# Forgetting attention with the softmax weights stationary: a single-product maximum pass, row sums from ones columns, and a turned result

## The chip, the cores and the metric

The kernel runs on one core of one Trainium2 chip. The metric is the device time of one execution in microseconds (us). The kernel before took 2423.89 us, the median of 3 runs (2420.24 to 2425.25). Differences of about 0.2% (5 us) are what a measurement of this kernel can tell from no change.

## The reference

One encoder layer over 2048 positions of width 1024. After a norm and one input projection, half of the columns go to a gated MLP over blocks of positions and half to eight attention heads of 64 dimensions. Then come an output projection, a norm, a feed-forward layer with a causal convolution of width 3, and a last norm. The change touches only the attention:

```python
def forgetting_attention(q, k, v, f_logit):
    ...
    c = jnp.cumsum(jax.nn.log_sigmoid(f_logit.astype(jnp.float32)), axis=1)
    ...
        s = jnp.einsum('bhtd,bshd->bhts', qi, k, preferred_element_type=jnp.float32) * scale
        s = s + ci[..., :, None] - c[:, :, None, :]
        s = jnp.where(kpos[None, :] <= qpos[:, None], s, -jnp.inf)
        p = jax.nn.softmax(s, axis=-1)
        return jnp.einsum('bhts,bshd->bthd', p.astype(v.dtype), v)
```

A query sees the keys up to itself. The logit is the scaled product plus a difference of two cumulative sums.

## The kernel before, in words

**Precision.** Every large product is made from operands split into a high and a low part in the 32-bit TensorE type fp32r (names ending in h or hi, and l or lo). A product then takes two or three matrix products.

**Order of the work.** A main stream of products runs from start to end: the projections (`phase_a`), the output projection (`c_half`, `c_late`), and the two halves of the feed-forward layer (`d_half`, `late_half`, `down`). The main helper `mm3` (line 205) issues its products at line 211, and every one of them gives a credit. When the credits reach a rate (3.5 to 4.4 products), one step of the attention is issued by the generator `b_stream`, with a higher priority. So attention is a second stream that is woven into the first. A scheduler then fixes the order on each engine when the program is built. Where the main stream needs the attention's result for a block of 512 queries, `need(tb)` (line 136) issues all steps still missing, and `load_mix` (line 874) reads that result back from DRAM. There are four blocks of queries, tb = 0 to 3. Blocks 0 and 1 have to be done before the output projection's second block of rows, and block 3 before its last one.

**A piece** is one head h and one block tb. It takes two passes.

- *First pass*, `b_max` (line 752). For each block of 512 keys up to the diagonal and each of the four groups of 128 queries, one step: scores with the queries in rows, by two products. Line 772 has 96 rows of contraction (high parts, the two cumulative sums, and constants), line 773 has 128 rows (the cross terms of high and low parts). DVE takes the minimum along the row (the scores are negated), line 776, or 778 with the mask on the diagonal. ACT takes exponentials against that minimum and adds them up (line 781). At the end the row maximum is put together, and the reciprocal of the row sum (lines 783 to 802). `turn` (line 804) transposes the maxima into rows of the query operand t1.
- *Second pass*, `b_mix` (line 812). For each chunk of 128 keys, one step: scores with the keys in rows and up to 512 queries in columns, by two products (lines 833, 834), the mask on the diagonal (837, DVE), the exponential into e (839, ACT), and its split into ph (844, ACT) and pl (845, DVE). Two or three steps later (`LAG`) the product with the values follows, `pv` (line 819): v, the 128 keys by 64 high and 64 low columns, is stationary. ph and then pl move through it, up to 512 columns each (lines 821, 822), and add to one PSUM bank `o` that holds head dimensions in rows and queries in columns.
- *End of a piece*. The high and low halves of `o` are added (856, 857). For every second head the reciprocals of two heads are broadcast and turned by four transposes (line 864), multiplied in, split and written to DRAM.

A diagonal block has four chunks with 512, 384, 256 and 128 columns. Counted over the program, each of the lines 772, 773, 821, 822, 833 and 834 has 224 products of 512 columns and 32 each of 384, 256 and 128.

**Buffers.** The PSUM bank tags that matter are `s` (3 banks for scores), `o` (1 bank) and `dn` (2 banks). Scores use the `dn` banks as well once `self.more` is set, during the first half of the feed-forward layer.

## Time and profile before

| what | value |
|---|---|
| median of 3 runs | 2423.89 us |
| profiled execution | 2419.3 us, span of its instructions 2417.5 us |
| PE busy (products) | 2392.8 us, 11288 products |
| PEld busy (weight loads) | 1998.3 us |
| DVE busy | 1764.8 us |
| ACT busy | 1355.3 us |
| GpSimd busy | 323.2 us |
| DMA engines | 47.9% of 16 engines' span in the main queue |

Each product on PE comes as two instructions, a weight load (PEld) that puts the stationary operand in place, and the product itself, which streams the moving operand. The trace writes the shape as moving columns, for instance 128x512. Durations of products overlap one another in the trace, so that their sum is longer than the span. What one product costs in a row of products is the distance from its start to the next start, or the distance between the weight loads.

### The profile page before, as it was taken

What the parts mean: (1) busy time and instruction counts of PE and PEld (TensorE: products, weight loads), DVE (VectorE), ACT (ScalarE), POOL (GpSimd) and SP (SyncE); (2) the same over time, 40 slices, a digit from 0 to 9 for tenths busy, and PEclk for the clock granted to TensorE, in tenths of its full rate; (3) what the DMA queues carried; (4) which work ended last, traced back from release to release, by engine and by line L of the source; (5) the groups of instructions that cost most, each with busy time, mean ns of one, the idle gap of its engine ahead of it and who ended that gap; (6) DMA issues with size and microseconds to landing.
All of it is one profiled execution on the core that took longest, in us unless ns stands there. A gap on an engine that the chain in (4) does not pass through costs nothing.

```text
span 2417.5 us, 33292 instructions
## 1 busy us (share of the span) xinstructions
PE 2392.8 (99%) x11288; PEld 1998.3 (83%) x11288; DVE 1764.8 (73%) x3108; ACT 1355.3 (56%) x2652; POOL 323.2 (13%) x315
## 2 busy tenths in 40 slices
PE   9999999999999999999999999999999999999998
PEld 7888888988888888888888888888888888888887
DVE  6447776665568778878878774598888877857875
ACT  4246767644456555767677764365555455454444
POOL 4114140100241221211111101100000000000001
PEclk9999999999999999999999999999999999999999
DMA  8673635668855444555445555312222238438633
GB/s 278 182 241 111 206 100 175 186 192 265 260 191 183 160 163 161 165 173 185 146 151 182 170 195 203 116 53 96 79 86 81 87 96 310 157 99 300 205 118 122
DMA packets 246042, 400.58 MB, mean 166 GB/s; under 512 B 51224, under 2 KB 110744, under 8 KB 244448
## 3 DMA queue, kind: packets, MB, share of 16 engines
q1 hardware_dynamic: 240832, 374.34, 47.9%
q0 software_dynamic: 5040, 24.12, 2.5%
q8 instruction: 89, 1.46, 0.2%
q14 instruction: 81, 0.66, 0.1%
HBM read 304.79 MB, written 93.72 MB: 165 GB/s over the span
## 4 chain that ended last, share of the span: by engine, by line
PE 87%; DMA 2%; DVE 1%; ACT 1%; issue 0%; POOL 0%; POOLq 0%; SPq 0%; ACTq 0%; DVEq 0%
PE mm L211 37%; PE D L1378 16%; PE A L1176 3%; PE A L1178 3%; PE A L1177 3%; PE o L822 3%; PE o L821 3%; PE s L773 2%; PE s L772 2%; PE s L834 2%; PE s L833 2%; PE B L1178 2%; PE B L1177 2%; PE B L1176 2%; PE C L1176 1%; PE C L1177 1%
## 5 line engine op out<-in xcount | busy, mean ns | idle before, releaser
L211 PE MATMUL mm<-tlo,whi 128*128 128x512 f32 x896 | 351.4, 392 | 0.0
L211 PE MATMUL mm<-thi,wlo 128*128 128x512 f32 x896 | 351.1, 392 | 0.0
L211 PE MATMUL mm<-thi,whi 128*128 128x512 f32 x896 | 350.5, 391 | 0.5 <-DVE vn L519 0.5
L211 PE MATMUL mm<-whi,thi 128*128 128x512 f32 (+2 forms) x768 | 275.9, 360 | 6.1 <-DVE vn L519 4.4
L211 PE MATMUL mm<-wlo,thi 128*128 128x512 f32 (+2 forms) x768 | 275.5, 359 | 2.2 <-DVE wlo L164 2.2
L211 PE MATMUL mm<-whi,tlo 128*128 128x512 f32 (+2 forms) x768 | 274.8, 358 | 0.0
L150 POOL TENSOR_SCALAR whi<-raw 128x1024 fp32r<-128x1024 f32 (+3 forms) x114 | 132.4, 1163 | 963.2 <-PE mm L211 741.5
L781 ACT ACTIVATE s<-s,part 128x512 f32<-128x512 f32 (+3 forms) x261 | 154.7, 593 | 145.3 <-DVE part L776 80.6
L211 PEld LDWEIGHTS mm<-thi,whi 128*128 128x128 f32 x896 | 168.4, 188 | 35.2 <-issue 0.7
L211 PEld LDWEIGHTS mm<-thi,wlo 128*128 128x128 f32 x896 | 168.5, 188 | 34.1
L211 PEld LDWEIGHTS mm<-tlo,whi 128*128 128x128 f32 x896 | 168.5, 188 | 33.7
L845 DVE TENSOR_TENSOR pl<-e,ph 128x512 fp32r<-128x512 f32 (+1 forms) x218 | 142.9, 662 | 69.6 <-ACT ph L844 40.5
L211 PEld LDWEIGHTS mm<-whi,thi 128*128 128x128 f32 x768 | 145.9, 190 | 26.3 <-DVE vn L519 4.6
L164 DVE TENSOR_TENSOR wlo<-raw,whi 128x1024 fp32r<-128x1024 f32 (+2 forms) x106 | 135.1, 1276 | 44.0 <-POOL whi L150 43.0
L839 ACT ACTIVATE e<-s 128x512 f32<-128x512 f32 (+1 forms) x222 | 114.5, 530 | 91.8 <-DVE s L837 44.0
L211 PEld LDWEIGHTS mm<-wlo,thi 128*128 128x128 f32 x768 | 145.9, 190 | 22.7 <-DVE wlo L164 3.4
L211 PEld LDWEIGHTS mm<-whi,tlo 128*128 128x128 f32 x768 | 145.9, 190 | 19.3
L844 ACT ACTIVATE ph<-e 128x512 fp32r<-128x512 f32 (+1 forms) x218 | 120.6, 563 | 38.7 <-PE o L821 36.6
L1378 PE MATMUL D<-wh,xh 128*128 128x512 f32 x368 | 140.8, 389 | 1.2 <-DVE xo L1479 1.2
L1378 PE MATMUL D<-wl,xh 128*128 128x512 f32 x368 | 141.4, 389 | 0.0
L1378 PE MATMUL D<-wh,xl 128*128 128x512 f32 x368 | 137.5, 389 | 0.0
L776 DVE TENSOR_REDUCE part<-s 128x1 f32<-128x512 f32 x149 | 98.6, 684 | 20.9 <-PE s L773 19.9
(1858 smaller groups left out, 5850.4 us busy)
## 6 DMA issues: line engine op xcount, KB each, us to landing
raw<-in_w_up_dram SPq DMA_DIRECT2D x72, 512.0 KB
m<-kx SPq DMA_DIRECT2D x134, 256.0 KB
m<-kx SPq DMA_DIRECT2D x160, 136.0 KB
x<-act SPq DMA_DIRECT2D x84, 256.0 KB
v<-vd SPq DMA_DIRECT2D x67, 256.0 KB
raw<-in_w_in_dram SPq DMA_DIRECT2D x28, 512.0 KB
raw<-in_w_out_dram SPq DMA_DIRECT2D x24, 512.0 KB
tw<-in_w_down_dram SPq DMA_DIRECT2D x11, 1024.0 KB
```

Of the source, the lines that this page charges most:

```text
L150: self.cast_ins = self.nc.gpsimd.tensor_scalar(out, in_, 1.0, 0.0, ALU.mult, ALU.add).ins
L164: nc.vector.tensor_tensor(lo, raw, f32(hi), op=ALU.subtract)
L211: self.last_mm = self.nc.tensor.matmul(ps, lhsT=a[k], rhs=b[k], start=i == 0, stop=i == 3 * n - 1).ins
L776: nc.vector.tensor_reduce(dst, ps, axis=AX.X, op=ALU.min)
L781: nc.scalar.activation(ps[:, :n], ps[:, :n], AF.Exp, scale=-1.0, bias=dst, accum_out=ls[:, tt, sb:sb + 1])
L839: nc.scalar.activation(e[:, c], ps[:, c], AF.Exp, scale=-1.0)
L844: nc.scalar.activation(ph[:, c], e[:, c], AF.Copy)
L845: nc.vector.tensor_tensor(pl[:, c], e[:, c], f32(ph[:, c]), op=ALU.subtract)
L1176: mm(ps, lhsT=xh[:, ks], rhs=yh[:, k, :], start=fresh and k == 0, stop=False, **kw)
L1177: mm(ps, lhsT=xh[:, ks], rhs=yl[:, k, :], start=False, stop=False, **kw)
L1178: mm(ps, lhsT=xl[:, ks], rhs=yh[:, k, :], start=False, stop=k == 3, **kw)
L1378: nc.tensor.matmul(bank[t], lhsT=x[i][:, ts], rhs=w[k], start=fresh and j == 0 and i + k == 0, stop=last and i == 1, **kw)
```

## The change

- *First pass*: line 773's product and the load of its operand m2 are gone, and so are line 781's exponentials and everything that made a row sum of them. One product of 96 rows and a minimum are left in each step.
- *Second pass*: the scores are made as before. In `pv` the stationary operand is now a group of 128 queries of ph or pl, and the values move: 130 columns for ph (64 high, 2 of ones, 64 low), 66 for pl (64 high, 2 of ones). Each chunk has up to four groups of queries, so up to eight products where there were two. The ones columns collect the row sum. The result has queries in rows and takes two PSUM banks. The product of pl with the low values, which was in before, is left out.
- *End of a piece*: reciprocals from the ones column, high and low halves added, one multiplication. For every second head the result itself is turned by four transposes.
- *Buffers*: scores 3 banks to 2 (with `dn` 5 to 4), `o` 1 to 2, both for one piece. Two v tiles of fixed place with the ones columns written once (a third when `more` is set). Each load of v is two DMAs.

The core of the diff:

```diff
-    "mm": 2, "tp": 2, "dn": 2, "s": 3, "o": 1,
+    "mm": 2, "tp": 2, "dn": 2, "s": 2, "o": 2,
...
-                nc.tensor.matmul(ps[:, :n], lhsT=t1[0:96, ts], rhs=m1[0:96, :n], start=True, stop=False)
-                nc.tensor.matmul(ps[:, :n], lhsT=t2[:, ts], rhs=m2[:, :n], start=False, stop=True)
+                nc.tensor.matmul(ps[:, :n], lhsT=t1[0:96, ts], rhs=m1[0:96, :n], start=True, stop=True)
...
-                nc.scalar.activation(ps[:, :n], ps[:, :n], AF.Exp, scale=-1.0, bias=dst, accum_out=ls[:, tt, sb:sb + 1])
                 yield
...
+        self.V.append(self.V.pop(0))
+        v = self.V[0]
+        for i in range(2):
+            self.dma(f32(v[:, :, 66 * i:66 * i + 64]),
+                     self.vd[hf][sl, h, 64 * i:64 * i + 64].rearrange("(c p) d -> p c d", p=P))
...
         def pv():
-            sc, c, v, ph, pl = late.pop(0)
-            nc.tensor.matmul(po[:, c], lhsT=v, rhs=ph[:, c], start=sc == 0, stop=False)
-            nc.tensor.matmul(po[:, c], lhsT=v, rhs=pl[:, c], start=False, stop=sc == ns - 1)
+            sc, j, v, ph, pl = late.pop(0)
+            for i in range(j, 4):
+                o, c = po[i // 2][:, i % 2, :], slice(i * P, (i + 1) * P)
+                with self.tc.issue_after(first) if sc == 0 and i % 2 else ExitStack():
+                    ins = nc.tensor.matmul(o, lhsT=ph[:, c], rhs=v[:, 0:130], start=sc == 0 and i % 2 == 0, stop=False,
+                                           skip_group_check=True).ins
+                if i % 2 == 0:
+                    first = ins
+                nc.tensor.matmul(o[:, 0:66], lhsT=pl[:, c], rhs=v[:, 0:66], start=False, stop=sc == 4 * tb + i,
+                                 skip_group_check=True)
...
+        for i, o in enumerate(po):
+            q = slice(2 * i, 2 * i + 2)
+            nc.vector.reciprocal(rr[:, q], o[:, :, 64])
+            nc.scalar.activation(op[:, q, :], o[:, :, 66:130], AF.Copy)
+            nc.vector.tensor_tensor(op[:, q, :], o[:, :, 0:64], op[:, q, :], op=ALU.add)
+        nc.vector.tensor_tensor(op, op, rr.unsqueeze(2).broadcast_to([P, 4, 64]), op=ALU.mult)
```

What stands on an engine in the built program is shown at two places, before and changed. The first place is on PE, in a piece of block tb = 1, where the products with the values of a chunk stand. Names: o is the result bank, ph and pl the split weights, v the values, s a bank of scores, m and t the key and query operands, mm the main stream. Before:

```order
L833 MATMUL s_1248_5477<-t1_49_401,m1_47_399 128x256
L821 MATMUL o_1216_5344<-ph_1221_5355,v_1218_5348 128x512
L822 MATMUL o_1216_5344<-pl_1222_5356,v_1218_5348 128x512
L821 MATMUL o_1216_5344<-ph_1225_5372,v_1218_5348 128x512
L822 MATMUL o_1216_5344<-pl_1226_5373,v_1218_5348 128x512
L834 MATMUL s_1248_5477<-t2_1125_4952,m2_1237_5428 128x256
```

Two chunks stand here with two products each, all 512 wide. The same part of a piece in the changed program, on PE:

```order
L832 MATMUL s_1043_4905<-t2_920_4379,m2_1038_4879 128x384
L815 MATMUL o_1013_4796<-v_52_405,ph_1036_4870 128x130
L815 MATMUL o_1014_4797<-v_52_405,ph_1036_4870 128x130
L819 MATMUL o_1013_4796<-v_52_405,pl_1037_4871 128x66
L815 MATMUL o_1013_4796<-v_52_405,ph_1036_4870 128x130
L819 MATMUL o_1013_4796<-v_52_405,pl_1037_4871 128x66
L819 MATMUL o_1014_4797<-v_52_405,pl_1037_4871 128x66
L815 MATMUL o_1014_4797<-v_52_405,ph_1036_4870 128x130
L819 MATMUL o_1014_4797<-v_52_405,pl_1037_4871 128x66
L831 MATMUL s_1047_4927<-t1_49_401,m1_47_399 128x256
```

One chunk now has eight products of 130 and 66 columns. Each has its own part of ph or pl as the stationary operand; products that read alike differ in the group of queries.

The second place is on PE in the output projection, where the main stream first needs the attention's result for block 1 (operands thi and tlo of the main products mm). Before:

```order
L211 MATMUL mm_1574_7213<-wlo_1452_6774,thi_1441_6749 128x512
L772 MATMUL s_1413_6585<-m1_48_400,t1_50_402 128x128
L773 MATMUL s_1413_6585<-m2_1412_6582,t2_1397_6491 128x128
L211 MATMUL mm_1574_7213<-whi_1451_6773,tlo_1443_6751 128x512
L772 MATMUL s_1414_6594<-m1_48_400,t1_50_402 128x256
L773 MATMUL s_1414_6594<-m2_1412_6582,t2_1397_6491 128x256
L211 MATMUL mm_1567_7159<-whi_1454_6779,thi_1441_6749 128x512
```

The last row is the first product that reads the rows of heads 4 to 7 of block 1. Ahead of it the attention is already in the first pass of block 2, and main products stand between its steps. The same place in the changed program, on PE:

```order
L819 MATMUL o_1156_5453<-v_51_403,pl_1193_5649 128x66
L186 MATMUL s_1210_5730<-ident_58,op_1153_5443 128x128 x4
L778 MATMUL s_1337_6645<-m1_48_400,t1_50_402 128x512
L778 MATMUL s_1338_6653<-m1_48_400,t1_50_402 128x512
L778 MATMUL s_1339_6660<-m1_48_400,t1_50_402 128x512
L778 MATMUL s_1340_6668<-m1_48_400,t1_50_402 128x512
L778 MATMUL s_1341_6676<-m1_47_399,t1_50_402 128x512
L778 MATMUL s_1342_6683<-m1_47_399,t1_50_402 128x512
L778 MATMUL s_1344_6693<-m1_47_399,t1_50_402 128x512
L212 MATMUL mm_1487_7279<-whi_1381_6861,thi_1368_6831 128x512
```

The last heads of block 1 (the transposes of their result, line 186) now stand seven products ahead of the main product that needs them. From there back, over four pieces, no main product stands between the attention's: 24 products of the first pass, 64 of the second pass's scores, 208 with the values, 32 transposes and 3 turns of maxima. A second stretch of the same kind stands ahead of the end of block 3: 12 of the first pass, 64 scores, 232 with the values, 8 transposes and a turn.

More of the change, by code (lines that the diff above doesn't have):

```diff
@@ L28 @@
 BIG = 1e30
+VW = 144
 RATES = [3.5, 4.0, 4.4, 3.6]
@@ L428, in first_keys @@
         def first_keys():
-            banks = [self.til(pp, [P, TB], F32, "mm") for _ in range(2)] + [self.scores([P, TB]) for _ in range(3)]
-            banks.append(self.til(self.bpp, [P, TB], F32, "o"))
+            banks = [self.til(pp, [P, TB], F32, "mm") for _ in range(2)] + [self.scores([P, TB]) for _ in range(2)]
+            banks += [self.til(self.bpp, [P, TB], F32, "o") for _ in range(2)]
             def mms(u, b, k):
@@ L732, in scores @@
     def scores(self, shape):
-        self.nscore = (self.nscore + 1) % 5
-        if self.more and self.nscore > 2:
+        self.nscore = (self.nscore + 1) % 4
+        if self.more and self.nscore > 1:
             return self.til(self.dpp, shape, F32, "dn")
```

57 lines of the change are left out of this document (20 added, 37 removed), and 4 rows, old and new, of the table BUFS.

## The prediction

> **What bounds the kernel now.** The page comes first.
>
> ```profile
> span 2417.5 us, 33292 instructions
> PE 2392.8 (99%) x11288; PEld 1998.3 (83%) x11288; DVE 1764.8 (73%) x3108; ACT 1355.3 (56%) x2652; POOL 323.2 (13%) x315
> PEclk9999999999999999999999999999999999999999
> ```
>
> PE is busy for 99% of the span at the full granted clock. That alone proves little, since products overlap in the trace, so the stretches come next: one with attention woven in, one of 512-column products alone.
>
> ```profile
> core 0: us, PE busy (x) PEld busy (x) DVE busy (x) ACT busy (x) POOL busy (x), PEclk, DMA share, GB/s
> 1000.00:1200.00 200.00, 200.00 (x914) 165.95 (x914) 163.20 (x323) 138.84 (x311) 29.36 (x28) 1.00 0.50 163
> 1600.00:1800.00 200.00, 200.00 (x884) 165.62 (x883) 170.49 (x214) 103.88 (x160) 0.00 (x0) 1.00 0.24 84
> ```
>
> In the second, 200 us for 884 products is 0.226 us each, with no gap. In the first there are 914, because some are narrower. So where attention runs, PE takes product after product, and what the change does to PE's row is what it does to the time. The prices of products of other widths come from the timeline of PE and of the weight loads, at a place where a diagonal block makes them narrow.
>
> ```profile
> 607.19 0.33 PE L833 MATMUL s<-t,m 128*128 128x384 f32 x1
> 607.54 0.28 PE L833 MATMUL s<-t,m 128*128 128x256 f32 x1
> 610.07 0.22 PE L833 MATMUL s<-t,m 128*128 128x128 f32 x1
> 610.13 0.28 PE L834 MATMUL s<-t,m 128*128 128x128 f32 x1
> 607.20 0.19 PEld L834 LDWEIGHTS s<-t,m 128*128 128x128 f32 x1
> 607.37 0.19 PEld L833 LDWEIGHTS s<-t,m 128*128 128x128 f32 x1
> 607.54 0.19 PEld L834 LDWEIGHTS s<-t,m 128*128 128x128 f32 x1
> 607.66 0.19 PEld L211 LDWEIGHTS mm<-whi,tlo 128*128 128x128 f32 x1
> 607.78 0.19 PEld L821 LDWEIGHTS o<-ph,v 128*128 128x128 f32 x1
> 608.01 0.19 PEld L211 LDWEIGHTS mm<-whi,thi 128*128 128x128 f32 x1
> 610.08 0.19 PEld L834 LDWEIGHTS s<-t,m 128*128 128x128 f32 x1
> 610.18 0.19 PEld L211 LDWEIGHTS mm<-whi,tlo 128*128 128x128 f32 x1
> 610.29 0.19 PEld L211 LDWEIGHTS mm<-whi,thi 128*128 128x128 f32 x1
> ```
>
> A load starts when the product before its own starts (607.20 against 607.19). So the distance from one load to the next is the slot of one product: 0.17 us for 384 columns (607.20 to 607.37 and on to 607.54), 0.12 for 256 (607.66, 607.78), 0.23 for 512 (608.01). For 128 columns it is 0.10 and 0.11 (610.08, 610.18, 610.29), and this no longer falls with the columns: half of 0.12 would be 0.06. Below 256 columns the slot is that of the weight load. A longer row of narrow products says the same.
>
> ```profile
> 371.69 1.72 PE L561 MATMUL tp<-vn,sw 128*128 128x128 f32 x14
> 373.16 0.47 PE L833 MATMUL s<-t,m 128*128 128x512 f32 x1
> 373.48 0.39 PE L834 MATMUL s<-t,m 128*128 128x512 f32 x1
> ```
>
> From 371.69 to 373.48 stand 14 products of 128 columns and one of 512: 1.79 - 0.23 = 1.56 us, 0.111 each.
>
> **The sum on PE.** Taken away are line 773's products and those of lines 821 and 822, each 224 of 512 columns and 32 of 384, 256 and 128: 224 x 0.226 + 32 x (0.17 + 0.12 + 0.105) = 50.6 + 12.6 = 63.3 us each. First pass -63.3, values -126.5, together -189.8 us.
>
> Added: a head has 24 full chunks with four groups of queries and four diagonal blocks with 4 + 3 + 2 + 1, so 136 groups, 1088 over eight heads, and 2176 products of 130 or 66 columns. The trace shows none as narrow as 66 and none of this pair. By columns alone (0.226/512 us each) they would take 0.057 and 0.029 us; by the slots above, each takes 0.105 to 0.111. I take 0.110: every product brings its own stationary operand, and the rows at 128 columns show the slot of a load whatever streams. That is 239.4 us (228.5 to 241.5 by the rows). Net on PE: +49.6 us (38.7 to 51.7). The turned result costs nothing here: four transposes for every second head, before and now.
>
> The Trainium skill, in "TensorE: Matmul & The Clock Gate", section "Back-to-back issue gap", gives for a stream of load and product pairs a sustained 81 ns at 128 columns. By it the 2176 would take an estimated 176 us and the sum would be about -14 us. The rows here, at 105 to 111 ns, do not agree, and I go by them.
>
> **Other work that goes or comes.** Line 781's exponentials, the loads of m2 in the first pass (80 of 256 KB) and the row-sum arithmetic were all beside PE: in 1000 to 1200 ACT is busy 139 of 200 us and the DMA engines half. They give nothing. The second DMA for each v (80 more issues on SP's queue, in place of the 80 for m2) and GpSimd's memsets of ones are hidden by the same room; if a v came late, the pv that waits for it would hold every main product queued behind it on PE. Both `o` banks belong to one piece, so the next piece's first pv waits for the small operations of the end, but its first pass and two steps lie between. I take nothing for these.
>
> **Where the cover goes: two stretches of attention alone.** The order shows that with fewer banks for scores the attention falls behind the main stream, and that ahead of the products that need block 1 it stands alone on PE for four pieces. There PE's row is not all that counts, because DVE has more work per piece.
>
> ```profile
> L845 DVE TENSOR_TENSOR pl<-e,ph 128x512 fp32r<-128x512 f32 x143 | 109.3, 770 | 45.5 <-ACT ph L844 33.2 <-PE o L822 10.3 <-ACT e L839 1.5
> L845 DVE TENSOR_TENSOR pl<-e,ph 128x384 fp32r<-128x384 f32 x27 | 15.0, 554 | 5.8 <-PE o L822 2.0 <-PE s L833 1.8 <-ACT ph L844 1.6
> L845 DVE TENSOR_TENSOR pl<-e,ph 128x256 fp32r<-128x256 f32 x28 | 12.7, 452 | 11.9 <-PE o L822 9.2 <-ACT ph L844 2.3
> L845 DVE TENSOR_TENSOR pl<-e,ph 128x128 fp32r<-128x128 f32 x20 | 6.6, 331 | 6.4 <-ACT ph L844 3.4 <-PE o L822 3.0
> L776 DVE TENSOR_REDUCE part<-s 128x1 f32<-128x512 f32 x149 | 98.6, 684 | 20.9 <-PE s L773 19.9
> L778 DVE CUSTOM_DVE_ANT_0 s<-s,mask 128x512 f32<-128x512 f32 x29 | 20.5, 705 | 10.6 <-PE s L773 9.8 <-ACT ln L530 0.4
> L778 DVE CUSTOM_DVE_ANT_0 s<-s,mask 128x128 f32<-128x128 f32 x26 | 7.8, 300 | 3.5 <-PE s L773 3.5
> L778 DVE DVE_READ_ACCUMULATOR2_ANT part<- 128x1 f32 x128 | 17.9, 139 | 0.0
> L837 DVE TENSOR_TENSOR s<-s,maskT 128x128 f32<-128x128 f32 x108 | 30.4, 293 | 22.4 <-PE s L834 21.8
> L807 DVE TENSOR_TENSOR t<-s,rowsel 8x512 fp32r<-8x512 f32 x30 | 20.5, 684 | 2.8 <-PE s L806 1.9
> L195 DVE SCALAR_TENSOR_TENSOR tlo<-dn,cols,thi 128x512 fp32r<-128x512 f32 x16 | 11.7, 744 | 3.4 <-ACT thi L194 3.4
> L789 DVE TENSOR_SCALAR m<-mx 128x4 fp32r<-128x4 f32 x32 | 7.6, 236 | 0.6
> L844 ACT ACTIVATE ph<-e 128x512 fp32r<-128x512 f32 x143 | 89.4, 634 | 12.4 <-PE o L821 10.9 <-DVE st L411 0.4 <-ACT st L191 0.3
> L839 ACT ACTIVATE e<-s 128x512 f32<-128x512 f32 x150 | 87.4, 597 | 59.0 <-PE s L834 31.5 <-DVE s L837 18.0 <-DVE pl L845 4.9
> ```
>
> First stretch, PE: 24 first-pass products 4.9 us, scores 4 x 2 x (5 x 0.226 + 0.395) = 12.2, values 208 x 0.11 = 22.9, 32 transposes and three turns 3.7: 43.7 us. DVE: the 32 pl 20 x 0.770 + 4 x (0.554 + 0.452 + 0.331) = 20.7; 16 masks x 0.293 = 4.7; 16 minima x 0.684 = 10.9; eight masked minima at about 0.64 (mean of 0.705 and 0.300, plus 0.139) = 5.1; six tlo of the main stream's norm x 0.744 = 4.5; three turns x 0.684 = 2.1; four ends of a piece, an estimated 1.5 each from the small rows (0.236 twice, 0.293 twice, and a multiplication near the 0.452 of 256 columns) = 6.0; two splits and two sets of maxima 2.8. Together 56.8 us. ACT has 1.23 us for a full chunk, 25 for the 20 and under 40 if the 12 narrow ones cost as much, so it is not the bound. PE waits 56.8 - 43.7 = 13 us.
>
> Second stretch, ahead of block 3's result: 12 first-pass steps in a row, DVE 8 x 0.684 + 4 x 0.64 = 8.0 us against 2.4 on PE, of which the score banks cover a step or two: 4 us. The two second passes behind it are PE's (1.33 us of PE for a full chunk against 1.23 of ACT and 0.77 of DVE).
>
> First passes that are still woven in: from 1000 to 1200 DVE is busy 163.2 of 200 us. Two steps, one of each pass, are now 2 x 0.81 of main products + 0.45 + 0.90 = 2.97 us, so DVE does 2.42 us in them, less 0.684, 0.77 and about 0.1 of masks leaves 0.43 a step for the main stream. After the change a first-pass step has 0.81 + 0.226 = 1.04 on PE and 0.684 + 0.43 = 1.11 on DVE. The 224 steps of blocks 2 and 3 could cost 224 x 0.07 = 16 us; the second passes give it back and the banks hold about a microsecond, so I take 2.
>
> A wait that goes is the first product with block 1's rows, which waited for its load:
>
> ```profile
> 663.14 0.50 PE L211 MATMUL mm<-whi,thi 128*128 128x512 f32 x1 [1.74 <-DMA thi<-mixh]
> ```
>
> It goes into the first stretch: -2. The sum is 49.6 + 13 + 4 + 2 - 2 = +66.6, on the profiled execution's 2419.3 us: 2486. The median of the runs before is 4.6 us above that execution; I put the forecast at 2487.
>
> **The rivals.**
>
> *Narrow products cost what they stream (faster).* If a load hid behind the loads around it, the 2176 would cost 1088 x (0.057 + 0.029) = 94 us, PE would get -96 us, and with the 17 us of waits the time would be 2340. With a slot between, such as the 81 ns above, it is 2419 - 14 + 15 = 2420. It decides from a slot of 189.8/2176 = 87 ns, or 80 ns with the waits. Against it stands every narrow pair in the rows; for it only that none is a pair of 130 and 66. Chance 0.06, of which 0.05 are beyond the bound.
>
> *No waits.* The stretches overlap better than the sums say, and only PE's row counts: 2419.3 + 38.7 to 51.7, about 2465. For it is that the DVE sum uses means with waits for other engines' memory traffic in them. Chance 0.20.
>
> *DVE becomes the bound in all first passes.* The 16 us are paid in full, and each piece of the first stretch adds a microsecond between passes, because a second pass cannot start before its maximum is turned: 2487 + 14 + 4 + 5 = 2510. For it are the two score banks in place of three; against it, that these steps stand among main products. Chance 0.16.
>
> My forecast has the remaining 0.58.
>
> **How the numbers follow.** The forecast's own range is 2470 to 2500. Reaching to the second and third rival gives 2454 to 2512; the faster case and some of the tails are left out. Faster by over 0.2% (5 us, what a measurement here can tell) 0.05, within it 0.01, slower 0.94.
>
> **What would show it.** Right, if the changed profile has 1216 more products, load distances of 0.105 to 0.11 us within a chunk's eight, and the rows of 130 and 66 columns at the same slot. Right, if PE has gaps of some 13 us in a stretch of about 57 us without main products, released by DVE. Wrong, if those distances are near 0.06, or if the time is off by more than the waits while the slots hold.

## The result, and the profile after

The changed kernel took 2548.87 us (median of 4 runs, 2546.07 to 2551.05), the kernel before 2422.06 us on the same chip (4 runs, 2419.61 to 2425.25). The ratio is 1.0524 (95% interval 1.051 to 1.0539). The forecast was 2487 us with a range of 2454 to 2512: the direction was right, the size was half, and the time lies outside the range. The profiled execution took 2547.18 us, its span 2545.5 us, against 2417.5 before: +128.0 us. One execution of one kernel below (without the late loads, 3087.67 us at a mean granted clock of 0.74, where that kernel's other three have 0.98) is left out of its median and its ratio.

The page of the changed kernel, in the lines that stand first in the prediction:

```profile
span 2545.5 us, 34973 instructions
PE 2495.9 (98%) x12504; PEld 2111.7 (83%) x12504; DVE 1768.5 (69%) x3116; ACT 1135.1 (45%) x1998; POOL 320.7 (13%) x318
PEclk9999999999579999999999999899999999999999
```

There are 12504 products, 1216 more, as counted. The share of PE is as good as before. What is new stands in the third line: in the slices from 636 to 764 us the granted clock is 0.5 and 0.7, and near 1600 us 0.8. Before, it was 0.9 or more in every slice.

The price of a narrow product is read from the weight loads, where full and narrow products take turns at the full clock (start, duration):

```profile
1338.00 0.19 PEld L815 LDWEIGHTS o<-v+_1868_9038,ph+_2337_11239 128*128 128x128 f32 x1
1338.11 0.19 PEld L819 LDWEIGHTS o<-v+_1868_9038,pl+_2338_11240 128*128 128x128 f32 x1
...
1338.78 0.19 PEld L815 LDWEIGHTS o<-v,ph 128*128 128x128 f32 x1
1338.89 0.19 PEld L819 LDWEIGHTS o<-v,pl 128*128 128x128 f32 x1
```

From 1338.00 to 1338.89 stand eight of them, 0.111 us each, whether 130 or 66 columns move. Over the whole trace the median distance between the loads is 0.112 us for both. With 0.1115 the 2176 products take 242.6 us, and PE's row is 242.6 - 189.8 = 52.8 us longer. The rest of the 128.0 us, 75.2, is not in the row.

It is in the two stretches without main products. The view of windows gives, for each, its length, PE busy, DVE busy, ACT busy and the granted clock. The first two rows below are the two stretches, from the first product of attention to the next main product; the other two are those shown of before.

```profile
630.80:722.30 91.50, 81.39 (x332) 67.86 (x330) 50.77 (x122) 39.01 (x80) 0.00 (x0) 0.58 0.38 109
1582.50:1646.10 63.60, 50.11 (x318) 43.50 (x316) 35.48 (x75) 40.58 (x80) 3.48 (x8) 0.83 0.32 94
1000.00:1200.00 200.00, 199.90 (x1050) 170.74 (x1048) 144.95 (x278) 88.25 (x164) 37.38 (x34) 1.00 0.42 138
1600.00:1800.00 200.00, 189.51 (x960) 159.41 (x960) 144.48 (x207) 115.51 (x199) 11.68 (x19) 0.96 0.27 88
```

The first stretch took 91.5 us. By the slots of its products, at full clock, PE needs 44.1 there; DVE is busy for 50.8 and ACT for 39.0. No engine accounts for the length. The second took 63.6 us for 42.5 us of slots. Together the two are 47.4 + 21.1 = 68.5 us longer than their slots. 52.8 + 68.5 = 121.3 of the 128.0 us. Of the 68.5, PE stands idle for 91.50 - 81.39 = 10.1 and 63.60 - 50.11 = 13.5 us; for the other 44.9 it is busy, with products that take longer than their slots. Where attention is woven in (1000 to 1200), PE stays full.

The chain of waits inside the first stretch, its shares by line and its longest loads (start, duration):

```profile
by line: PE o L815 22.3%; PE o L819 15.7%; PE s L831 13.9%; PE s L832 10.4%; DMA m<-kx 8.0%; PE s L778 7.0%; DMA tlo<-mixl 6.1%; DVE part L781 4.5%; DMA t<-cc 2.7%; PE s L186 2.4%; PE dn L186 1.9%; DVE s L783 1.7%; issue 1.6%; DVE op L859 1
...
632.94 4.06 DMA m<-kx
641.71 2.49 DMA t<-cc
675.81 3.27 DMA m<-kx
719.85 5.55 DMA tlo<-mixl
```

Loads of keys (m) and of a query's cumulative sum (t) stand in the chain, 10.7% of 91.5 = 9.8 us. The load of the attention's result (thi and tlo) comes last. The tlo in the last row lands at 725.40, after the stretch; what PE waits for at the end of the two stretches is thi:

```profile
722.31 0.80 PE L212 MATMUL mm<-whi,thi 128*128 128x512 f32 x1 [0.60 <-DMA thi<-mixh]
1646.10 0.80 PE L212 MATMUL mm<-whi,thi 128*128 128x512 f32 x1 [6.62 <-DMA thi<-mixh]
```

The 6.62 us for block 3's result are new. Before, the one wait of PE for such a load was the 1.74 us for block 1's. The remainder of the first stretch's chain is PE's, but at which clock? The load of t at 641.71 shows how the clock goes. On PE:

```profile
642.63 0.42 PE L815 MATMUL o<-v,ph 128*128 128x130 f32 x2
644.33 0.94 PE L778 MATMUL s<-m,t 96*128 96x512 f32 x2 [1.28 <-DMA t<-cc]
```

PE waited 1.28 us for the load, at 644.6 us the granted clock fell to half, and it stayed there for 85.3 us:

```profile
640.00:660.00 20.00, 16.84 (x74) 13.82 (x72) 12.32 (x33) 8.27 (x18) 0.00 (x0) 0.62 0.32 86
660.00:680.00 20.00, 16.38 (x57) 13.13 (x57) 10.80 (x30) 5.01 (x12) 0.00 (x0) 0.50 0.39 116
680.00:700.00 20.00, 20.00 (x79) 18.14 (x79) 7.66 (x17) 11.42 (x23) 0.00 (x0) 0.50 0.30 80
700.00:720.00 20.00, 17.73 (x67) 15.07 (x67) 10.00 (x23) 6.70 (x16) 0.00 (x0) 0.50 0.47 130
```

From 680 to 700 PE is busy all the time and has only 79 products, where the row of 1000 to 1200 has 105 in 20 us. A busy PE at half clock looks like a full one: only the clock column tells. Between the first 70 us and the last 5 us of the execution, the trace's record of the clock has 119.5 us at half, in five pieces; before, it has none there.

The Trainium skill has a rule for this, in "TensorE: Matmul & The Clock Gate", section "HAM oscillation — how this bites in real kernels": no idle gaps of PE over about 3.4 us. Here a gap of 1.28 us was enough, so this trace does not bear the rule out as a bound; the section behind it, "A second HAM failure mode: psum-queue depth-cycling", where PE idles for short times between groups of products and the clock goes up and down, is the nearer one.

### The profile page after: what moved, and what is told of

Same layout as the page of the kernel before. It is cut to its first block, busy times and chain, and to the rows that moved or that the text cites. A ratio compares the mean times of both kernels' runs of the same rounds, so it can differ in the third digit from the quotient of the medians.

```text
span 2545.5 us, 34973 instructions
## 1 busy us (share of the span) xinstructions
PE 2495.9 (98%) x12504; PEld 2111.7 (83%) x12504; DVE 1768.5 (69%) x3116; ACT 1135.1 (45%) x1998; POOL 320.7 (13%) x318
## 4 chain that ended last, share of the span: by engine, by line
PE 87%; DVE 4%; DMA 3%; issue 3%; ACT 2%; POOL 1%; SPq 0%; POOLq 0%; DVEq 0%; ACTq 0%
PE mm L212 38%; PE D L1379 14%; PE o L815 5%; PE o L819 3%; PE A L1177 3%; PE A L1179 3%; PE A L1178 3%; PE s L831 2%; PE s L832 2%; PE s L778 2%; PE B L1178 2%; PE B L1179 2%; PE B L1177 2%; DMA x<-in_xT_dram 1%; PE C L1178 1%
## 5 line engine op out<-in xcount | busy, mean ns | idle before, releaser
L151 POOL TENSOR_SCALAR whi<-raw 128x1024 fp32r<-128x1024 f32 (+3 forms) x114 | 127.1, 1117 | 980.8 <-PE mm L212 872.0
L837 ACT ACTIVATE e<-s 128x512 f32<-128x512 f32 (+2 forms) x214 | 110.1, 526 | 152.5 <-PE s L832 93.4
L815 PE MATMUL o<-v,ph 128*128 128x130 f32 x688 | 176.4, 304 | 0.0
L819 PE MATMUL o<-v,pl 128*128 128x66 f32 x688 | 150.8, 257 | 1.6 <-DVE pl L843 1.6
L815 PEld LDWEIGHTS o<-v,ph 128*128 128x128 f32 x688 | 137.6, 207 | 10.3 <-ACT ph L842 0.7
## 6 DMA issues: line engine op xcount, KB each, us to landing
v<-vd SPq DMA_DIRECT2D x132, 128.0 KB
```

Source lines behind the costliest of these rows:

```text
L151: self.cast_ins = self.nc.gpsimd.tensor_scalar(out, in_, 1.0, 0.0, ALU.mult, ALU.add).ins
L815: ins = nc.tensor.matmul(o, lhsT=ph[:, c], rhs=v[:, 0:130], start=sc == 0 and i % 2 == 0, stop=False, skip_group_check=True).ins
L819: nc.tensor.matmul(o[:, 0:66], lhsT=pl[:, c], rhs=v[:, 0:66], start=False, stop=sc == 4 * tb + i, skip_group_check=True)
L837: nc.scalar.activation(e[:, c], ps[:, c], AF.Exp, scale=-1.0)
```

## The experiments

Theories at first. **A:** fewer score banks let attention fall behind in the built order; where it then stands alone, PE waits, and the waits bring the clock down. **B:** the narrow products themselves bring it down. Later **C**: the clock falls after a window of about 3.4 us in which columns stream through PE for under 0.4 of the time, and returns only after a fuller one. Then **D:** loads of keys and queries that come late make the waits. "Slots beyond" below means the length of the stretches with over 6 us of slots in which no main product stands, less the slots of their products.

**Two score banks and nothing else.** The kernel before, with

```diff
-    "mm": 2, "tp": 2, "dn": 2, "s": 3, "o": 1,
+    "sx": 1, "mm": 2, "tp": 2, "dn": 2, "s": 2, "o": 1,
...
-        self.nscore = (self.nscore + 1) % 5
-        if self.more and self.nscore > 2:
+        self.nscore = (self.nscore + 1) % 4
+        if self.more and self.nscore > 1:
```

> The kernel before with two score banks in place of three (four in place of five with dn; the spare bank is used once at the start and then idle); every product is as before. In the built order attention now stands alone on PE for stretches of 35, 21 and 68 us of slots. Theory A (fewer score banks make attention fall behind; alone on PE it waits for DVE and ACT, and the waits bring the granted clock to half): the clock falls to half in those stretches and the time rises by 40 to 110 us over before, with the slots unchanged. Theory B (it is the narrow products, which stream a small share of their slots, that bring the clock down): there are none here, so the clock stays at 1.00 after the start and the time rises by less than 25 us, for waits alone.

Measured: 2541.37 us (2540.3 to 2543.96), ratio 1.049 (1.0475 to 1.0506). With no narrow product in it, taking one bank away costs almost what the whole change costs. The two long stretches:

```profile
638.20:718.20 80.00, 60.14 (x185) 36.13 (x183) 45.25 (x104) 49.62 (x116) 0.00 (x0) 0.72 0.44 132
1525.40:1641.30 115.90, 87.89 (x332) 62.20 (x330) 73.68 (x149) 92.28 (x212) 3.47 (x8) 0.85 0.41 128
```

They are 80.0 and 115.9 us long for 34.6 and 68.0 us of slots, again with no engine full. A is right as to the stretches and the clock, though the rise of 118 us is above its 40 to 110; B falls as the only cause.

**pl on 130 columns.** The changed kernel with wider products of the same slot:

```diff
-                nc.tensor.matmul(o[:, 0:66], lhsT=pl[:, c], rhs=v[:, 0:66], start=False, stop=sc == 4 * tb + i,
+                nc.tensor.matmul(o, lhsT=pl[:, c], rhs=v[:, 0:130], start=False, stop=sc == 4 * tb + i,
```

> The changed kernel with 130 columns for pl as well as for ph (it adds the product of pl with the low values, which the changed kernel leaves out). Order and number of products stay. Theory A: a slot of 0.111 us holds 130 columns as it holds 66, so the time stays at 2549 within 10 us, with the same half-clock stretches. Theory B: the share of a slot in which PE streams rises from about 0.37 to 0.49, the half-clock stretches get shorter, and the time falls by 20 to 60 us.

Measured: 2534.44 us (2524.88 to 2536.7), ratio 1.0452 (1.0423 to 1.0482), 14 us less, with 71.7 us at half clock. The first stretch:

```profile
630.00:711.40 81.40, 70.00 (x332) 55.88 (x330) 49.87 (x122) 37.63 (x80) 0.00 (x0) 0.71 0.43 122
```

It has the same slots, 30.7 us less at half clock, and is 10.1 us shorter: a third of a microsecond for each. The fall of the time lies between the two theories' numbers (within 10 us, or 20 to 60 us); the shorter half clock is as B had it, with products, order and slots unchanged.

**One result bank, three score banks.** The changed kernel with 128 columns a group (two of the low columns of v are left out), so that one bank holds the result:

```diff
-    "mm": 2, "tp": 2, "dn": 2, "s": 2, "o": 2,
+    "mm": 2, "tp": 2, "dn": 2, "s": 3, "o": 1,
...
-        po = [self.til(pp, [P, TB], F32, "o")[:, 0:260].rearrange("p (a c) -> p a c", c=130) for _ in range(2)]
+        pb = self.til(pp, [P, TB], F32, "o").rearrange("p (a c) -> p a c", c=128)
+        po = [pb[:, 0:2, :], pb[:, 2:4, :]]
```

> The changed kernel with 128 columns a group in place of 130, so that the result takes one bank and the scores have three again (it leaves out two of the 64 low columns of the values). As many products as changed, 8 to each chunk; in the built order no stretch of attention alone is over 15 us of slots, where the changed kernel has 44 and 43. Theory A: the clock stays at 1.00 after the start, and the time is that of before plus the slots, 2420 + 50, so 2465 to 2485. Theory B: the narrow products still bring the clock down, 2520 to 2550.

Measured: 2488.16 us (2480.57 to 2492.82), ratio 1.0266 (1.0243 to 1.029). The long stretches are gone from the order, slots beyond are 8.6 us, half clock 27.3 us. The time is 3 us above A's range and far under B's. By the spans (+67.8 against +128.0), 60 of the change's 128 us belong to the banks.

**The first pass alone.** The kernel before with one product in the first pass; the exponentials stay, so that the row sums lack the cross terms.

```diff
-                nc.tensor.matmul(ps[:, :n], lhsT=t1[0:96, ts], rhs=m1[0:96, :n], start=True, stop=False)
-                nc.tensor.matmul(ps[:, :n], lhsT=t2[:, ts], rhs=m2[:, :n], start=False, stop=True)
+                nc.tensor.matmul(ps[:, :n], lhsT=t1[0:96, ts], rhs=m1[0:96, :n], start=True, stop=True)
```

> The kernel before with one product in the first pass (exponentials and row sums kept, so the row sums lack the cross terms of high and low parts), three score banks, the products with the values as before. Both theories: 320 products go, 63 us of slots, no stretch of attention alone, clock 1.00: 2355 to 2365. If it falls by much less, the price of the first pass in my sum was wrong.

Measured: 2357.12 us (2355.66 to 2358.86), ratio 0.9729 (0.9714 to 0.9743).

```profile
PE 2329.6 (99%) x10968; PEld 1942.6 (83%) x10968; DVE 1755.9 (75%) x3108; ACT 1353.5 (57%) x2652; POOL 320.5 (14%) x315
PEclk9999999999999999999999999999999999999999
```

Its span is 2354.4 us, 63.1 under that of before; the sum had -63.3. This is as expected, and the version beats both kernels.

**Sums collected in the wide product.** One product and a maximum in the first pass, three score banks, and the row sums without narrow products: v stays stationary, with the ones columns in place of two low columns (which are left out), and up to 512 queries move. The result is turned twice, by 128 more transposes.

```diff
-            late.append((sc, c, v4[:, sc % 4, :], ph, pl))
+            late.append((sc, c, v4[:, sc % 4, 0:P], ph, pl))
...
+            o = self.transpose4(None, "s", [os[:, i * P:(i + 1) * P] for i in range(4)]).rearrange("p (a c) -> p a c", c=P)
+            nc.vector.reciprocal(rr, o[:, :, 64])
```

> A version meant to keep the gain of the first pass without narrow products: one product and a maximum in the first pass, three score banks, values stationary and 512 columns moving as in the kernel before, with two ones columns among the values in place of two of the 64 low columns (which it leaves out). The result is copied and turned by four transposes for each head, normalised, and turned back as in the changed kernel; both turns are issued a few steps later. Slots: 63 us of the first pass go, 128 transposes come (14 us), so 2422 - 49 = 2373. In the built order attention stands alone for 12 and 24 us. If only waits and slots count: 2375 to 2385. If a stretch of that length takes the clock down as well: up to 2400.

Measured: 2405.14 us (2404.2 to 2408.47), ratio 0.9928 (0.9913 to 0.9943), 5 us above the 2400 that was expected if the clock falls as well: two stretches of 12.3 and 23.8 us of slots took 25.2 and 44.9.

**The values alone.** The kernel with one result bank, with the second product back in the first pass and still no exponentials (the two low columns stay left out).

```diff
-                nc.tensor.matmul(ps[:, :n], lhsT=t1[0:96, ts], rhs=m1[0:96, :n], start=True, stop=True)
+                nc.tensor.matmul(ps[:, :n], lhsT=t1[0:96, ts], rhs=m1[0:96, :n], start=True, stop=False)
+                nc.tensor.matmul(ps[:, :n], lhsT=t2[:, ts], rhs=m2[:, :n], start=False, stop=True)
```

> The kernel of e3 (three score banks, 128 columns a group) with both products in the first pass again, still without exponentials there: the second part of the change alone. Slots: 241 - 126.5 = 114 us more than before, so 2536 if the clock holds, as the built order has no stretch of attention alone over 15 us; one or two drops of the clock, as in e3, would add 7 to 14 us: 2530 to 2552. If narrow products cost more than their slots, above 2560.

Measured: 2541.66 us (2540.35 to 2546.63), ratio 1.0493 (1.0477 to 1.0508), as expected. Its span is 123.3 us above before, of which 242.6 - 126.5 = 116.1 are slots; slots beyond are 4.6.

**One result bank and a wide pl.** In the kernel with one result bank, pl moves 128 columns in place of 66.

```diff
-                nc.tensor.matmul(o[:, 0:66], lhsT=pl[:, c], rhs=v[:, 0:66], start=False, stop=sc == 4 * tb + i,
+                nc.tensor.matmul(o, lhsT=pl[:, c], rhs=v[:, 0:128], start=False, stop=sc == 4 * tb + i,
```

> The kernel of e3 with 128 columns for pl too. Slots and order as e3 within a few us. Theory C (the clock falls after a stretch of about 3.4 us in which PE streams columns for less than some 0.4 of the time; narrow products hold that share near 0.5, so that a small wait is enough, and it comes back only after a share above some 0.75): the share rises with the columns, at least one of e3's two drops goes or gets shorter, 2470 to 2484. If the columns do not matter: 2488 within 5 us.

Measured: 2481.23 us (2480.9 to 2485.35), ratio 1.0243 (1.0228 to 1.0259), 17.1 us at half clock against 27.3. It lies where C put it, but the intervals of the two ratios overlap.

**Two banks, filled with the step's own operands.** The kernel with two score banks and 320 added products of 512 columns in the first pass:

```diff
+                nc.tensor.matmul(self.til(self.bpp, [P, TB], F32, "sx"), lhsT=t1[0:96, ts], rhs=m1[0:96, :], start=True, stop=True)
```

> The kernel of e1 (before with two score banks) with one more product of 512 columns in each step of the first pass, into the spare bank, read by nobody: 320 products, 72 us of slots more. Its stretches of attention alone are 44, 84 and 76 us of slots. Theory C: the added columns keep the streamed share up, the clock holds or drops for much shorter times, and the waits are partly filled: 2541 + 72 - 55 (clock) - 15 to 40 (waits), 2518 to 2545, so no slower than e1. If the clock follows the waits or the stretches themselves: 2541 + 72 - 15 at best, 2590 to 2615.

Measured: 2630.03 us (2628.02 to 2632.2), ratio 1.0853 (1.0835 to 1.0872): 89 us more than with two banks alone, not fewer, and above both expectations. Each added product reads the step's keys and queries, so that the waits moved in front of it (23.8 us of PE's waits for keys stand right ahead of the added products) and were not filled. Half clock stayed at 109.2 us. The expectation failed, and the run tells nothing about C.

**Two banks, filled with constants.** So the added product reads constants only, and stands behind a step's scores, in the pieces that stand alone:

```diff
...
+    def keep_busy(self, h, tb):
+        if tb == 1 and h > 3 or tb == 3 and h > 2:
+            with self.tc.issue_after(self.last_sc):
+                self.nc.tensor.matmul(self.sx[:, :512], lhsT=self.mask[:, 0:P], rhs=self.mask[:, :512], start=True, stop=True)
...
```

> This is the kernel with two score banks (the first experiment, 2541 us, 109 us of it at half clock) with one added product per attention step, right behind the step's scores, in the last four pieces of block 1 and the last five of block 3, which are the ones that stand alone on PE in the built order. The added product reads two constants only and writes a bank that nobody reads, so it waits for nothing; it streams 512 columns. There are 224 of them, about 153 inside the stretches that stand alone, 71 among main products. The stretches stay where they were. Theory C (the clock goes down when PE streams too small a part of a 3.4 us window): the added products fill idle time of PE, the clock stays up for most of it, half clock under 50 us; the 71 cost 71 x 0.226 = 16 us, the 153 cost little, and up to 54 us of the clock's price come back: 2500 to 2535, in spite of more work. Rival (the waits as such bring the clock down, or the added work simply adds to the row): half clock stays near 109 us, and the time is 2541 + 16 to 51 = 2557 to 2592.

> The same kernel as the one with 224 added products of 512 columns, in the same places, but each streams 64 columns. A product of that width takes 0.11 us of PE's row and streams for about 0.03. Theory C: the share of a window in which columns stream rises by a few hundredths only, so the clock goes down nearly as without them, half clock 80 to 110 us; the 71 among main products cost 8 us, those in the stretches little: 2535 to 2560. So by theory C the kernel with the larger added products is the faster of the two. Rival (any product that shortens the gaps keeps the clock up, whatever it streams): half clock under 50 us and 2495 to 2525. If the waits as such decide, both have about 109 us at half clock, and this one is the faster by the work that it lacks, 224 x 0.115 = 26 us.

Measured: with 512 columns 2555.93 us (2552.71 to 2558.75), ratio 1.054 (1.0524 to 1.0556), with 64 columns 2550.91 us (2548.29 to 2553.51), ratio 1.0521 (1.0503 to 1.0539). The two long stretches, first with 512 columns:

```profile
639.00:718.10 79.10, 63.68 (x226) 36.80 (x228) 45.16 (x104) 49.27 (x116) 0.00 (x0) 0.83 0.45 134
1532.10:1651.90 119.80, 97.97 (x420) 63.62 (x426) 72.56 (x150) 93.46 (x212) 3.47 (x8) 0.95 0.40 125
```

and with 64:

```profile
639.40:720.10 80.70, 63.40 (x230) 37.97 (x229) 45.25 (x104) 49.33 (x116) 0.00 (x0) 0.74 0.44 135
1531.80:1649.30 117.50, 90.04 (x427) 59.40 (x425) 72.34 (x147) 92.06 (x211) 3.48 (x8) 0.91 0.40 125
```

The same number of products in the same places leaves 54.6 us at half clock when 512 columns stream and 92.2 when 64 do (109.2 with none). So the number of products does not hold the clock, and a short product in each gap does little. A product of 512 columns also takes twice the slot of one of 64, so this pair alone does not tell columns from busy time; that 130 columns for pl, at unchanged slots, cut the half clock from 119.5 to 71.7 us speaks for the columns, as C has it. On the time C failed with 512 columns: it had that kernel as the faster of the two, and it is 5 us slower. The two long stretches hardly changed in length, though 54.6 us of half clock were gone in all. Either half clock costs little there, or what it gave back the added work took; these two runs can't tell.

**Without the late loads.** The changed kernel, and the kernel with two score banks, without the loads of keys and queries in the pieces that stand alone:

```diff
...
+        self.keep = keep = tb == 1 and h > 3 or tb == 3 and h > 2
+        if not keep:
+            self.t2 = self.til(self.mp, [P, TB], F32R, "t2")
+            self.dma(f32(t1[0:64, :]), self.qx[hf][h, 0:64, sl])
...
+        if not keep:
+            self.dma(f32(m1[0:68, :]), self.kx[hf][h, 64:132, sl])
```

> The changed kernel without the loads of keys and queries (m1, m2, t1, t2) in the last four pieces of block 1 and the last five of block 3, those that stand alone on PE: they work on the keys and queries that lie in the buffers from the pieces before, with the exponent scaled to nothing in the second pass. So the attention of these pieces is left out as to its values; the instructions on PE, ACT and DVE stay as they are, and so do the stretches in the built order (43 and 39 us of slots). In the trace of the changed kernel the first stretch takes 91.5 us for 44.1 us of slots, the second 63.6 for 42.5, and the chain of waits in them has loads of keys and queries for 8.0% + 2.7% and 11.7%, that is 9.8 and 7.4 us, each load 2.5 to 4.2 us long. Theory D (loads that the attention needs sooner than they come, with two buffers each, make the waits, and these bring the clock down): 17 us go at once, and with the clock some more, up to 25: 2505 to 2532, half clock well under 119 us. Rival E (the chain from engine to engine in each step, over two score banks and two buffers of ph and pl, sets the length, and the loads only lie in it): 0 to 8 us go, 2540 to 2549.

> The kernel with two score banks and nothing else changed (the first experiment, 2541 us), without the loads of keys and queries in the same nine pieces, whose attention is thereby left out as to its values. Its stretches alone took 80.0, 115.9, 18.1 and 35.7 us for 131.9 us of slots, and the chain in the two long ones has loads of keys and queries for 14.8% and 21.9%, 11.8 and 25.4 us. Theory D: 37 us go and up to 15 more with the clock: 2488 to 2506. Rival E: 0 to 12 us go, 2529 to 2541.

Measured: the changed kernel 2529.76 us (median of three, 2527.28 to 2531.34), ratio 1.0443 (1.0426 to 1.046), 19.1 us less. The kernel with two banks 2499.58 us (2496.84 to 2500.78), ratio 1.0321 (1.0304 to 1.0339), 41.8 us less. Both are where D put them. With the loads in, the chain in the second long stretch of the two-bank kernel began with

```profile
by line: DMA m<-kx 21.9%; PE o L822 8.1%; PE o L821 7.1%; PE dn L833 6.0%; PE dn L834 4.7%; ACT e L839 4.4%; issue 4.3%; PE s L833 4.1%; ACT ph L844 4.0%; PE dn L772 4.0%; PE s L772 3.7%; DMA thi<-mixh 3.1%; PE s L834 3.0%; ACT s L781 2.4%;
```

25.4 us of loads of keys in 115.9. Without them the two stretches of that kernel, and the first of the changed one, were:

```profile
632.50:705.50 73.00, 55.00 (x187) 34.41 (x185) 46.08 (x107) 51.06 (x119) 0.00 (x0) 0.79 0.25 77
1502.90:1597.60 94.70, 79.75 (x327) 53.50 (x325) 71.80 (x149) 89.73 (x210) 3.48 (x8) 0.96 0.19 57
```

```profile
628.90:710.20 81.30, 73.55 (x329) 61.25 (x327) 48.22 (x116) 37.14 (x78) 0.00 (x0) 0.62 0.22 60
```

In the two-bank kernel's last stretch ACT is now busy for 89.7 of 94.7 us: without the loads, an engine sets its length. In the changed kernel's first one none does; its clock is still 0.62.

**Scores twice, in the first stretch.** More work that streams more columns, in the changed kernel and in the one without the late loads:

```diff
...
+            if tb == 1 and h > 3:
+                nc.tensor.matmul(ps[:, c], lhsT=m1[:, ks], rhs=t1[:, c], start=True, stop=True)
             nc.tensor.matmul(ps[:, c], lhsT=m1[:, ks], rhs=t1[:, c], start=True, stop=False)
```

> The changed kernel, in which the last four pieces of block 1 make the first product of each scores step twice into the same bank (in the first pass the only one, in the second pass that with m1), the second time over the first. Nothing is left out; 64 products are added, 12.4 us of slots, 8.3 of them inside the first stretch that stands alone on PE (52.5 us of slots there, 44.1 without), the rest ahead of it among main products; the other stretches stay. In the changed kernel this stretch takes 91.5 us, 77.7 of them at half clock. If the half clock costs there what it seems to, a third to half a microsecond for each one (the kernel with 130 columns for pl had 30.7 us less at half in it and was 10.1 shorter), and the added columns keep the clock up, the stretch has under 40 us at half and takes 70 to 82 us, in spite of more work: 2534 to 2545 in all. Rival, the half clock costs next to nothing, as the kernels with the added products and two score banks showed: 91.5 plus 0 to 8 us for the stretch, 4 outside: 2553 to 2561. If the clock is no better for it (70 us or more at half), the price stays open.

> The same doubling of 64 products in the changed kernel without the loads of keys and queries in the nine pieces (whose attention is so left out as to its values), 2530.6 us: there the first stretch takes 81.3 us, 61.2 at half clock, for 43.4 us of slots, and loads are no part of it. With the doubled products it has 50.3 us of slots; 5.6 stand outside. If the half clock costs a third to half a microsecond for each one and the added columns keep it up: under 30 us at half in the stretch, which takes 62 to 74 us, 2516 to 2529 in all. If it costs next to nothing: 81 to 88 us and 2536 to 2543.

Measured: 2544.7 us (2541.73 to 2547.71), ratio 1.0505 (1.0487 to 1.0522), and 2524.59 us (2521.44 to 2528.84), ratio 1.0423 (1.0408 to 1.0439): 4 and 6 us less, with 12.4 us more work in PE's row. The first stretch, in the changed kernel with the loads and then without:

```profile
635.80:716.00 80.20, 72.30 (x377) 58.07 (x375) 49.77 (x120) 37.95 (x80) 0.00 (x0) 0.76 0.44 123
```

```profile
636.30:709.60 73.30, 66.66 (x362) 54.74 (x360) 46.81 (x114) 35.24 (x74) 0.00 (x0) 0.79 0.24 67
```

From 91.5 to 80.2 us, with 39.0 us less at half clock (77.7 to 38.7) and 8.3 us more of slots; without the loads from 81.3 to 73.3, with 30.2 less (61.2 to 31.0) and 6.7 more. So in these stretches a microsecond at half clock costs 11.3/39.0 = 0.29 if the added products were free, and (11.3 + 8.3)/39.0 = 0.50 if they cost their slots; the other pair gives 0.26 and 0.49. The rival (next to nothing) falls for this stretch; in the two-bank kernel the price was not measured. The Trainium skill, in "TensorE: Matmul & The Clock Gate", section "HAM oscillation — how this bites in real kernels", counts the penalty at half of the throttled time; the pairs here lie at that or below.

**All runs in one account.** Slots added to PE's row, and slots beyond, against the difference of the spans from that of before (us). The slots come from 0.226, 0.1115 and the sums above.

| kernel | span less 2417.5 | slots | slots beyond | left | at half clock |
|---|---|---|---|---|---|
| changed | +128.0 | +52.8 | 68.5 | 6.7 | 119.5 |
| two score banks | +122.2 | 0 | 117.8 | 4.4 | 109.2 |
| pl on 130 columns | +113.6 | +52.8 | 56.7 | 4.1 | 71.7 |
| one result bank | +67.8 | +52.8 | 8.6 | 6.4 | 27.3 |
| first pass alone | -63.1 | -63.3 | 0 | 0.2 | 0 |
| sums in the wide product | -10.8 | -49.1 | 34.0 | 4.3 | 37.5 |
| values alone | +123.3 | +116.1 | 4.6 | 2.6 | 13.7 |
| one bank, wide pl | +62.1 | +52.8 | 9.3 | 0.0 | 17.1 |
| two banks, step's operands | +211.1 | +72.3 | 134.7 | 4.1 | 109.2 |
| two banks, 512 constants | +135.3 | +50.6 | 82.8 | 1.9 | 54.6 |
| two banks, 64 constants | +130.8 | +24.9 | 98.4 | 7.5 | 92.2 |
| changed, no late loads | +110.5 | +52.8 | 48.2 | 9.5 | 92.2 |
| two banks, no late loads | +77.6 | 0 | 71.0 | 6.6 | 47.8 |
| changed, scores twice | +125.9 | +65.2 | 50.5 | 10.2 | 88.8 |
| no late loads, scores twice | +103.7 | +65.2 | 33.4 | 5.1 | 54.7 |

Two numbers leave 0 to 10 us of every span: the row of PE, and what the stretches of attention alone take beyond it. This tells where the time is, not why, since the slots beyond are read from the same traces. The added products of 512 and 64 columns have 16-bit operands; their slots are taken at the prices of the others (one that stands among main products takes 0.23 and 0.12 us).

## Why the prediction was wrong in size

- **The sum on PE held.** A narrow product takes 0.111 to 0.112 us, where 0.110 was taken, and +49.6 was +52.8. Each half holds by itself: the first pass measured -63.1 in the span (-63.3 worked out), the values +123.3 with 4.6 us of stretches (239.4 - 126.5 = +112.9 worked out).
- **Woven-in first passes held.** From 1000 to 1200 PE is busy for 199.90 of 200 us. The rival in which DVE bounds all first passes falls.
- **The step that failed is "PE waits 56.8 - 43.7 = 13 us", and the 4 us of the second stretch.** They were 47.4 and 21.1. The sums themselves were near (PE 44.1 for 43.7, DVE 50.8 for 56.8), but the step took the longest engine for the length of the stretch. PE's gaps in the first stretch, 10.1 us of which DVE released 6.6, are even near the 13, but not by that sum, since DVE was busy for only 50.8 of 91.5 us. Most of the time is not in gaps at all: products took 81.4 us for 44.1 us of slots. Four things were left out.
  - The row of PE was priced at the full clock. 99.6 us of the two stretches are at half clock, worth 26 to 50 us by the 0.26 to 0.50 above.
  - Loads of keys and queries that the woven stream hid are late when attention runs alone: 19.1 us with what follows from them, the clock's part included.
  - The main stream waits for the load of block 3's result, 6.62 us.
  - The chain from engine to engine is still there. Without late loads and with the doubled scores, slots beyond are 33.4 us: 40.0 us at half clock account for 10 to 20, PE's waits for the results' loads (0.91 and 6.27) for 7.2. The 6 to 16 left are below the 17 that the prediction had for the two stretches.
- **The banks were named and mispriced.** The prediction had the smaller number of score banks as the reason for the stretches. What this costs it did not see: slots beyond of 117.8 us in the kernel before with two score banks, 60 us of the span in the changed kernel. Why less there is open. The exponentials of the first pass, which read a score bank once more in the kernel before (PE waited 10.8 us for line 781 in the kernel with two banks), may be a part of it; no run tests that.
- **"A wait that goes" went in part.** The wait for block 1's result was 1.74 us before; now PE waits 0.60 us for its high part and 0.53 for its low part. The wait for block 3's result, taken at nothing, is larger than what went.
- **Taken at nothing:** loads were given nothing because the room in 1000 to 1200 hides them; in the stretches that cover is gone. No load of v stands in the chain's rows, though each is two DMAs now.

The forecast had no case with a lower clock, so no rival came near the time. Open is how the 68.5 us divide between clock, loads and chain to better than these bounds, since each brings the others with it.

## What to carry to other kernels

When a change makes a woven-in stream fall behind, price the stretch in which it then stands alone by its chain: the loads that nothing hides any more, then the hand-overs, and only last the longest engine. Read the clock column of such a stretch, since a PE at half clock looks full in the busy share. A PSUM bank given to one use has a price in another: here one score bank cost the kernel before as much as the whole change, and the banks were 60 of the 128 us of the change itself. The single product of the first pass, which needs no further bank, is a gain of 2.7% by itself (with row sums that lack the cross terms).

## What the hardware showed that was not expected

- The granted clock falls to half after waits far under 3 us (1.28 us in the case above). What counts, the windows ahead of the falls tell in part. Every time at half clock is a multiple of 3.41 us (3.4, 13.7, 85.3 in the changed kernel), so the profiled executions of all 16 kernels were cut, from 100 us on, into windows of that length, in step with the falls. The columns of the products that start in a window, at 0.226/512 us each, give the share of it that streams:

| streamed share | windows at full clock | followed by half clock |
|---|---|---|
| under 0.25 | 28 | 28 |
| 0.25 to 0.35 | 40 | 28 |
| 0.35 to 0.45 | 60 | 17 |
| 0.45 to 0.50 | 72 | 4 |
| 0.50 and over | 10774 | 0 |

- So the share decides at both ends, and C's bound of 0.4 is a middle value: between 0.25 and 0.50 a fall may follow or not. One product of 512 columns more or less in a window is 0.07 of the share.
- The clock returns late. By the same count (columns at their full-clock price), none of the 119 half-clock windows with a share under 0.30 was the last one, and all 39 with 0.50 or more were. From 680 to 700 us PE was busy throughout, with a share of 0.33, and stayed at half.
- The slot of a narrow product is 0.111 us at 66, 128 and 130 columns alike.
